# Some feed-forward block pairs of a three-product float32 kernel computed by Strassen's seven half-sized products

## The chip, the core and the metric

The kernel runs on one core of one Trainium2 chip. The metric is the device time of one execution in microseconds (us): the median of three runs of the kernel before is 2325.37 us (2324.46 to 2325.86).

## What is computed

The reference takes x (1 x 512 x 1024, float32) through a first block (RMSNorm, attention, gates, and an MLP with a squared ReLU, 1024 to 4096 to 1024) and through two layers of feed-forward, mixer, feed-forward. The feed-forwards are SwiGLUs of width 1408:

```
x = x + jnp.square(jax.nn.relu(h2 @ w_up[l])) @ w_down[l]      # the MLP

def _swiglu(u, wi, wo):
    a, g = jnp.split(u @ wi, 2, axis=-1)
    return (jax.nn.silu(a) * g) @ wo                           # four calls, u = rms_norm(x)
```

## The kernel before

Activations lie with features on the partitions and the 512 positions along the row, in eight feature blocks (k = 0 to 7). A float32 product is made of three: each operand is split into a high part (`xh`, `whi`, a cast) and a low part (`xl`, `wlo`, the difference), and `mm3` (L389) issues high by high, high by low, low by high into one bank of PSUM.

A weight tile is loaded raw by SyncE's queue (`wraw`, 2 buffers, L382), cast by ScalarE into `whi` (L384, 4 buffers) and subtracted by VectorE into `wlo` (L385). The norm of a row enters late: the products run on x times its gain, and each result is multiplied by the row `Rrow` (L467) once `norm_job` (L496) has made it from a sum of squares (`ssq`), a reciprocal root and two helper products (`dg`, `bcps`); results that are ready sooner are held.

`swiglu` (L570) makes 11 blocks j of 128 features. Each loads two chunks of weights (k 0 to 3 and 4 to 7), multiplies into `pa` and `pg` with `fm` (24 matmuls of 512 columns each), and hands over to an evacuation: VectorE `t1` (L582) and `t2` (L584), ScalarE Silu (L583), GpSimd `t2 * t1` (L585), then ScalarE's cast `hidh` (L562) and VectorE's difference `hidl` (L563). `mlp` (L609) works in three groups of 11, 11 and 10 blocks, two blocks to a load, with `pu` and a square (L625 to L628), and after each group `down` (L592) multiplies by the second matrix into `pd` and adds to x (L480). `down` is the last reader of a group's `hid` places, which come from a store `H` of 22 places of 4 KB a row. Scratch tiles (`scr`) rotate through 6 places, PSUM through 8 banks.

TensorE runs in the order in which the program is written, with other jobs put in at `turn()`. The order of the other engines is set by the scheduler at build time; each of them then runs its own list in order.

Of the kernel before, what the change touches and what calls it, by code (L numbers as in the profile page):

```python
# [28 lines left out]
def dram(t, off, ap):  # L29
    return bass.AP(tensor=t.tensor, offset=t.offset + off, ap=ap)  # L30
# [125 lines left out]
class Net:  # L156
# [44 lines left out]
        return self.ps.tile([128, S], F32, name=name, tag="ps")  # L201


    def mm(self, out, lhsT, rhs, start, stop):
        self.nc.tensor.matmul(out, lhsT, rhs, start=start, stop=stop)  # L205
        n = 1
        for d in rhs.shape[1:]:
            n *= d
        self.loom.now += n * 4.17e-4 if rhs.dtype == F32R else 2 * max(0.107, n * 8.34e-4)
# [176 lines left out]
            out += [(hi[:, k * w_:(k + 1) * w_], lo[:, k * w_:(k + 1) * w_]) for k in range(kn)]  # L386
        return out

    def mm3(self, ps, whi, wlo, xhi, xlo, first, last):  # L389

        self.mm(ps, whi, xhi, first, False)
        self.mm(ps, whi, xlo, False, False)
        self.mm(ps, wlo, xhi, False, last)

    def mm3t(self, ps, whi, wlo, xhi, xlo, first, last):

# [146 lines left out]
    def square(self, tb, t, ssq):  # L543
        A = self.nc.scalar
        junk = self.H.get("xj", [128, D])
        A.activation(junk, t, AF.Square, accum_out=ssq[:, tb:tb + 1])
        self.H.put(junk, t)

    def x_tok_job(self, out):
        for tb in range(TB):  # L550
            yield lambda: self.H.room(4096)
            t = self.H.get("xtok", [128, D])
            for h in range(2):
                ps = self.bank("xtp")
                for k in range(4):
                    self.tr(ps[:, k * 128:(k + 1) * 128], self.x[:, h * 4 + k, tb * 128:(tb + 1) * 128], self.ident)
                self.nc.scalar.copy(t[:, h * 512:(h + 1) * 512], ps)
            out.append(t)
            yield 10.0

    def split_to(self, hi, lo, t):
        self.nc.scalar.copy(hi, t)  # L562
        self.nc.vector.tensor_sub(lo, t, hi.bitcast(F32))  # L563


    def hid(self, n):
        hp = [self.pair("hid") for _ in range((n + 1) // 2)]
        return hp, self.blocks(hp, n)

    def swiglu(self, wi):  # L570
        nc = self.nc
        hp, hid = self.hid(11)
        for j in range(11):
            parts = self.load_w(wi, 2 * FFN, 0, KB, j * 128, 128, FFN + j * 128)
            pa, pg = self.bank("pa"), self.bank("pg")
            self.fm(parts, self.xs, 0, pa)
            self.fm(parts, self.xs, 1, pg)

            def evac(j=j, pa=pa, pg=pg):
                t1 = self.scr("t1")  # L580
                t2 = self.scr("t2")
                nc.vector.tensor_mul(t1, pa, self.rrow)  # L582
                nc.scalar.activation(t1, t1, AF.Silu)  # L583
                nc.vector.tensor_mul(t2, pg, self.rrow)  # L584
                nc.gpsimd.tensor_mul(t2, t2, t1)  # L585
                self.split_to(hid[j][0], hid[j][1], t2)
            self.hold(evac)
        return hp, hid

    def down(self, hid, wo, r0, scale, norm):  # L590
        n = len(hid)
        for c in range(4):  # L592
            parts = self.load_w(wo, D, r0, n, c * 256, 256)
            for i in range(2):
                ps = self.bank("pd")
                self.fm(parts, hid, i, ps)
                self.update_x(2 * c + i, ps, scale, norm)

    def down_tok(self, hid, wo, out, xtok):
        nc = self.nc  # L600
        for c in range(2):
            def evac(b, ps):
                o = self.scr("oo")
                cs = slice(c * 512, c * 512 + 512)
                nc.vector.scalar_tensor_tensor(o, ps, 0.5, xtok[b][:, cs], op0=ALU.mult, op1=ALU.add)
                nc.sync.dma_start(out[0, b * 128:(b + 1) * 128, cs], o)
            self.tm(wo, D, 0, hid, c * 512, 512, evac)

    def mlp(self, wu, wd, g_next):  # L609
        nc = self.nc  # L610
        j0 = 0
        for gi, n in enumerate((11, 11, 10)):
            hp, hid = self.hid(n)
            j = 0
            while j < n:
                w = min(2, n - j)
                parts = self.load_w(wu, 4096, 0, KB, (j0 + j) * 128, 128 * w)
                for i in range(w):
                    ps = self.bank("pu")
                    self.fm(parts, self.xs, i, ps)  # L620

                    def evac(ps=ps, hi=hid[j + i][0], lo=hid[j + i][1]):
                        r = self.scr("r")
                        q = self.scr("rq")
                        nc.vector.scalar_tensor_tensor(r, ps, 0.0, self.rrow, op0=ALU.max, op1=ALU.mult)  # L625
                        nc.gpsimd.tensor_mul(q, r, r)
                        nc.scalar.activation(hi, r, AF.Square)
                        nc.vector.tensor_sub(lo, q, hi.bitcast(F32))  # L628
                    self.hold(evac)
                j += w  # L630
            if gi == 2:
                self.g = g_next
            self.down(hid, wd, j0 * 128, 1.0, gi == 2)
            self.H.put(*sum(hp, ()))
            j0 += n

# [126 lines left out]
    def block1(self):  # L763
# [82 lines left out]
        def two(c0, c1, order, tabs, keys):  # L846

            ts = [self.tok("qk") for _ in range(2)]

            def ev(b, ps):  # L850
                for i in range(2):
                    nc.scalar.activation(ts[i][:, b], ps[:, i * 256:i * 256 + 256], AF.Copy,
                                         scale=rc[:, order * 4 + b:order * 4 + b + 1])
            self.tm(w, IN_WIDTH, 0, self.xs, c0, 256, ev, order, c1)
            for i in range(2):
                heads(ts[i], order, tabs[i], keys[i], T_HEADS[i])
# [212 lines left out]
    def ffn2(self, l, which, g_next, last=False):  # L1069
        a = self.a  # L1070
        wi, wo = a[f"ffn{which}_wi_2"][l], a[f"ffn{which}_wo_2"][l]
        xtok = []
        if which == 1:
            b = a["b_in_2"][l]
            self.lcols = self.columns("lcols", [(dram(b, 0, []), 2), (dram(b, 256, []), 2), (dram(b, 768, []), 8),
                                                (dram(b, 3240, []), 24), (a["ml_conv_b_2"][l], 8), (a["ml_conv_w_2"][l], 32),
                                                (a["mla_q_norm_2"][l], 2), (a["mla_kv_norm_2"][l], 1)], 30.0)
        if last:
            self.loom.add(self.x_tok_job(xtok))
        hp, hid = self.swiglu(wi)  # L1080
        if last:
            self.loom.wait(lambda: len(xtok) == TB)
            self.down_tok(hid, wo, a["out"], xtok)
            return
        self.g = g_next
        self.down(hid, wo, 0, 0.5, True)
        self.H.put(*sum(hp, ()))
# [190 lines left out]
    def mla_job(self, l, c4t, c4, ssc, gq, gkv, y, ready):  # L1278
# [322 lines left out]
    def ml_attn(self, qkt, qk, wt, vml, got, ys, ready):  # L1601
# [33 lines left out]
        def fin():  # L1635
# [69 lines left out]
WB = (2, 4)  # L1705
```

## Time and profile before

| what | before |
|---|---|
| median of 3 runs | 2325.37 us |
| the profiled execution | 2324.79 us |
| its span, first to last instruction | 2323.1 us |
| TensorE busy | 2308.8 us, 99% |
| weight loads busy (beside the matmuls) | 1913.4 us, 82% |
| VectorE busy | 1293.6 us, 56% |
| ScalarE busy | 907.3 us, 39% |
| GpSimd busy | 381.3 us, 16% |
| granted TensorE clock | 1.0 of full |

The profile is one execution's record. An engine's busy share is an average over all stages; a wait that counts is one that ends last for TensorE. Matmuls overlap in the pipeline, so their pace is read from start to start and not from the length of one.

### The profile page before, as it was taken

To read this page: it belongs to the slowest core of one execution; us is meant where nothing else is said; L and a number is where in the kernel's file an instruction comes from. 1 tells how busy PE (TensorE), PEld (TensorE's weight loads), DVE (VectorE), ACT (ScalarE), POOL (GpSimd) and SP (SyncE) were. 2 spreads that over 40 slices of the span, in tenths; PEclk is the share of its full clock that TensorE was granted. 3 is DMA by queue.
4 is the path that set the end of the run, shared out by engine and by line. 5 is a ranking of instruction groups with operands and counts; after the bars stand their busy time and mean duration, and the time that the engine had idled before them with its cause. 6 is when DMAs were issued, how large, how long until landed. Compare 5 with 4: busy or idle time off the path is not lost.

```text
span 2323.1 us, 28438 instructions
## 1 busy us (share of the span) xinstructions
PE 2308.8 (99%) x10884; PEld 1913.4 (82%) x10884; DVE 1293.6 (56%) x2255; ACT 907.3 (39%) x1509; POOL 381.3 (16%) x385
## 2 busy tenths in 40 slices
PE   8999999999999999999999999999999999999999
PEld 7898888888888888877888888888888778888887
DVE  7844556444355545678564555455457674646552
ACT  6655432222223233656533333223236672333331
POOL 2000024101022112111111311211211101213110
PEclk9999999999999999999999999999999999999999
DMA  4223333233323323313323333333233142323332
GB/s 139 65 64 87 105 100 93 91 99 101 98 86 105 99 89 95 102 55 91 105 64 91 109 91 91 100 92 100 91 102 91 46 114 73 88 83 105 93 100 87
DMA packets 250524, 213.68 MB, mean 92 GB/s; under 512 B 14230, under 2 KB 234132, under 8 KB 250388
## 3 DMA queue, kind: packets, MB, share of 16 engines
q1 hardware_dynamic: 250388, 211.87, 30.6%
q8 instruction: 85, 1.39, 0.2%
q14 instruction: 51, 0.42, 0.1%
HBM read 208.64 MB, written 3.19 MB: 91 GB/s over the span
## 4 chain that ended last, share of the span: by engine, by line
PE 98%; DVE 1%; DMA 0%; ACT 0%; issue 0%; SPq 0%; ACTq 0%
PE pgate L205 15%; PE pd L205 15%; PE pt L205 14%; PE pg L205 10%; PE pa L205 10%; PE pu L205 8%; PE pf L205 6%; PE po L205 6%; PE pbr L205 5%; PE mls L205 1%; PE mnum L205 1%; PE sbl L205 1%; PE mss L205 1%; PE dio L205 1%; PE s L205 1%; PE pT L212 0%
## 5 line engine op out<-in xcount | busy, mean ns | idle before, releaser
L385 DVE TENSOR_TENSOR wlo<-wraw,whi 128x1024 fp32r<-128x1024 f32 (+3 forms) x394 | 550.8, 1398 | 414.1 <-ACT whi L384 409.8
L384 ACT CAST whi<-wraw 128x1024 fp32r<-128x1024 f32 (+3 forms) x394 | 404.3, 1026 | 657.2 <-PE pg L205 141.7
L205 PE MATMUL pd<-hidh,wlo 128*128 128x512 f32 x520 | 202.4, 389 | 0.0
L205 PE MATMUL pd<-hidl,whi 128*128 128x512 f32 x520 | 202.4, 389 | 0.0
L205 PE MATMUL pd<-hidh,whi 128*128 128x512 f32 x520 | 202.4, 389 | 0.0
L205 PE MATMUL pgate<-xh,whi 128*128 128x512 f32 x512 | 201.5, 394 | 0.0
L205 PE MATMUL pgate<-xh,wlo 128*128 128x512 f32 x512 | 199.6, 390 | 0.0
L205 PE MATMUL pgate<-xl,whi 128*128 128x512 f32 x512 | 199.4, 389 | 0.0
L205 PE MATMUL pt<-whi,xh 128*128 128x512 f32 (+2 forms) x480 | 182.2, 380 | 0.1
L205 PE MATMUL pt<-whi,xl 128*128 128x512 f32 (+2 forms) x480 | 172.5, 359 | 0.0
L205 PE MATMUL pt<-wlo,xh 128*128 128x512 f32 (+2 forms) x480 | 172.3, 359 | 0.0
L205 PE MATMUL pa<-xl,whi 128*128 128x512 f32 x352 | 137.3, 390 | 0.7 <-DVE xl L474 0.7
L205 PE MATMUL pa<-xh,whi 128*128 128x512 f32 x352 | 137.7, 391 | 0.0
L205 PE MATMUL pg<-xh,whi 128*128 128x512 f32 x352 | 137.5, 391 | 0.0
L205 PE MATMUL pa<-xh,wlo 128*128 128x512 f32 x352 | 137.2, 390 | 0.0
L205 PE MATMUL pg<-xh,wlo 128*128 128x512 f32 x352 | 137.1, 390 | 0.0
L205 PE MATMUL pg<-xl,whi 128*128 128x512 f32 x352 | 137.1, 389 | 0.0
L585 POOL TENSOR_TENSOR t<-t,t 128x512 f32<-128x512 f32 x44 | 56.8, 1290 | 426.5 <-ACT whi L384 303.8
L205 PEld LDWEIGHTS pd<-hidl,whi 128*128 128x128 f32 x520 | 97.6, 188 | 20.4
L205 PEld LDWEIGHTS pd<-hidh,whi 128*128 128x128 f32 x520 | 97.6, 188 | 20.2
L205 PEld LDWEIGHTS pd<-hidh,wlo 128*128 128x128 f32 x520 | 97.6, 188 | 20.1
L205 PEld LDWEIGHTS pt<-whi,xh 128*128 128x128 f32 x480 | 102.7, 214 | 13.0 <-issue 3.0
(519 smaller groups left out, 4612.8 us busy)
## 6 DMA issues: line engine op xcount, KB each, us to landing
wraw<-in_w_in_dram SPq DMA_DIRECT2D x116, 512.0 KB
wraw<-in_ffn_wi_dram SPq DMA_DIRECT2D x176, 256.0 KB
wraw<-in_ffn_wo_dram SPq DMA_DIRECT2D x34, 512.0 KB
wraw<-in_w_up_dram SPq DMA_DIRECT2D x32, 512.0 KB
wraw<-in_w_out_dram SPq DMA_DIRECT2D x24, 512.0 KB
wraw<-in_w_down_dram SPq DMA_DIRECT2D x24, 512.0 KB
wraw<-in_w_in_dram SPq DMA_DIRECT2D x32, 256.0 KB
wraw<-in_ffn_wo_dram SPq DMA_DIRECT2D x12, 384.0 KB
```

Of the source, the lines that this page charges most:

```text
L205: self.nc.tensor.matmul(out, lhsT, rhs, start=start, stop=stop)
L384: nc.scalar.copy(hi, raw)
L385: nc.vector.tensor_sub(lo, raw, hi.bitcast(F32))
L585: nc.gpsimd.tensor_mul(t2, t2, t1)
```

## The change

For 23 pairs of blocks the 48 matmuls of 512 columns are replaced by seven products of 12 matmuls of 256 columns. The two halves of the positions and the two halves of k make the quarters A11, A12, A21, A22 of the activations; two blocks c0 and c1 and the same halves of k make the four quarters of the weights. In a SwiGLU the pair is `pa` and `pg` of j = 3, 5, 7, 9; in the MLP it is two neighbouring blocks, seven times.

`forms` (once in each SwiGLU and once in the MLP, five calls) makes the four sums of activation quarters S2, N1, S3, S4 and splits them: per call 4 scaled copies on ScalarE (128x256), 16 scalar_tensor_tensor on VectorE (128x256), 8 casts and 8 differences (128x512). `load_sums` loads a pair's raw weights into two places of `H` of their own (`sraw`, not `wraw`), makes the sums `tA` and `tB` by four VectorE adds (128x512), and splits E11, E21 with E22, T2 with T4, and T1 with T3 into the four buffers of `whi` and `wlo`: 512 + 3 x 1024 columns where a pair had 2 x 1024. `seven` runs the products in the order A11 E11, S4 E22, A12 E21, S2 T2, A22 T4, N1 T1, S3 T3. The third adds into the bank of the first, and before it ScalarE copies that bank (`A.copy(s1, a)`, tile `m7`). Places for `hid` are taken pair by pair. In the last SwiGLU the transposes of x move to j = 10.

```diff
+    def forms(self):
+        nc, g, H = self.nc, self.g, self.H
+        V, A = nc.vector, nc.scalar
+        ng = self.tiny.tile([128, KB], F32, name="ng", tag="ng")
+        V.tensor_scalar(ng, g, -1.0, None, op0=ALU.mult)
+        names = ("S2", "N1", "S3", "S4")
+        self.sums = {n: tuple(H.get("sum" + n, [128, 4, 256], F32R) for _ in range(2)) for n in names}
+        half = slice(0, 256), slice(256, 512)
+        for i in range(2):
+            f = {n: self.scr("f" + n).rearrange("p (k c) -> p k c", c=256) for n in names}
+            t = self.scr("ft").rearrange("p (k c) -> p k c", c=256)
+            for j in range(2):
+                k1, k2 = 2 * i + j, 4 + 2 * i + j
+                x = lambda k, h: self.x[:, k, half[h]]
+                A.activation(t[:, j], x(k1, 1), AF.Copy, scale=g[:, k1:k1 + 1])
+                for n, k, h, sc, other in (("N1", k2, 1, g, t), ("S2", k1, 0, ng, f["N1"]), ("S3", k1, 0, g, t),
+                                           ("S4", k2, 0, ng, f["S2"])):
+                    V.scalar_tensor_tensor(f[n][:, j], x(k, h), sc[:, k:k + 1], other[:, j], op0=ALU.mult, op1=ALU.subtract)
+            for n in names:
+                hi, lo = (y[:, 2 * i:2 * i + 2] for y in self.sums[n])
+                self.split_to(hi, lo, f[n])
+        q = lambda k, h: [(self.xh[:, kk, half[h]], self.xl[:, kk, half[h]]) for kk in range(4 * k, 4 * k + 4)]
+        self.quarters = {"A11": q(0, 0), "A12": q(1, 0), "A22": q(1, 1)}
+        for n in names:
+            self.quarters[n] = [(self.sums[n][0][:, k], self.sums[n][1][:, k]) for k in range(4)]
...
+    def load_sums(self, w, ncol, c0, c1):
+        nc, H = self.nc, self.H
+        V, A = nc.vector, nc.scalar
+        E = []
+        for k0 in (0, 4):
+            raw = H.get("sraw", [128, 1024])
+            rv = raw.rearrange("p (k h c) -> p k h c", h=2, c=128)
+            for h, c in ((0, c0), (1, c1)) if c1 != c0 + 128 else ((None, c0),):
+                n = 128 if h is not None else 256
+                nc.sync.dma_start(rv[:, :, h] if h is not None else raw.rearrange("p (k c) -> p k c", c=256),
+                                  dram(w, k0 * 128 * ncol + c, [[ncol, 128], [128 * ncol, 4], [1, n]]))
+            E.append((raw, rv))
+        (r1, v1), (r2, v2) = E
+        ta, tb = (H.get(n, [128, 2, 4, 128]) for n in ("tA", "tB"))
+        V.tensor_add(ta[:, 1], v1[:, :, 1], v2[:, :, 1])
+        V.tensor_add(tb[:, 0], ta[:, 1], v1[:, :, 0])
+        V.tensor_add(tb[:, 1], tb[:, 0], v2[:, :, 0])
+        V.tensor_add(ta[:, 0], v1[:, :, 0], v1[:, :, 1])
+        out = {}
+        def split(src, n, names, pick):
+            hi = self.wp.tile([128, n], F32R, name="whi", tag="whi", bufs=WB[1])
+            lo = self.wp.tile([128, n], F32R, name="wlo", tag="wlo", bufs=WB[1])
+            self.split_to(hi, lo, src)
+            for i, name in enumerate(names):
+                out[name] = [tuple(y[:, o:o + 128] for y in (hi, lo)) for o in (pick(i, k) for k in range(4))]
+        flat = lambda t: t.rearrange("p a k c -> p (a k c)")
+        e11 = self.wp.tile([128, 512], F32R, name="whi", tag="whi", bufs=WB[1])
+        f11 = self.wp.tile([128, 512], F32R, name="wlo", tag="wlo", bufs=WB[1])
+        h11, l11 = (y.rearrange("p (k c) -> p k c", c=128) for y in (e11, f11))
+        A.copy(h11, v1[:, :, 0])
+        V.tensor_sub(l11, v1[:, :, 0], h11.bitcast(F32))
+        out["E11"] = [(e11[:, k * 128:k * 128 + 128], f11[:, k * 128:k * 128 + 128]) for k in range(4)]
+        split(r2, 1024, ("E21", "E22"), lambda i, k: k * 256 + i * 128)
+        split(flat(tb), 1024, ("T2", "T4"), lambda i, k: i * 512 + k * 128)
+        split(flat(ta), 1024, ("T1", "T3"), lambda i, k: i * 512 + k * 128)
+        H.put(ta, tb, r1, r2)
+        return out
...
+    def seven(self, w, ncol, c0, c1, u, v, done):
         nc = self.nc
-        hp, hid = self.hid(11)
+        V, A = nc.vector, nc.scalar
+        W = self.load_sums(w, ncol, c0, c1)
+        a, b, c, d, e = (self.bank("ps7")[:, 0:256] for _ in range(5))
+        m = self.scr("m7")
+        s1, u2 = m[:, 0:256], m[:, 256:512]
+        u3 = self.scr("u7")[:, 0:256]
+        def prod(ps, q, e, first):
+            for k in range(4):
+                self.mm3(ps, *W[e][k], *self.quarters[q][k], first and k == 0, k == 3, skip_group_check=not first)
+            self.loom.turn()
+        prod(a, "A11", "E11", True)
+        A.copy(s1, a)
+        prod(e, "S4", "E22", True)
+        prod(a, "A12", "E21", False)
+        prod(b, "S2", "T2", True)
+        V.tensor_add(u2, b, s1)
+        prod(d, "A22", "T4", True)
+        V.tensor_add(u2, e, u2)
+        prod(c, "N1", "T1", True)
+        V.scalar_tensor_tensor(v[:, 0:256], c, -1.0, u2, op0=ALU.mult, op1=ALU.subtract)
+        prod(b, "S3", "T3", False)
+        V.tensor_add(u3, b, s1)
+        V.scalar_tensor_tensor(v[:, 256:512], c, -1.0, u3, op0=ALU.mult, op1=ALU.subtract)
+        V.tensor_add(u[:, 256:512], d, u3)
+        done(a)
+    def swiglu(self, wi, last):
+        V, A, G = nc.vector, nc.scalar, nc.gpsimd
+        hp, hid = [], []
         for j in range(11):
+            self.more_hid(hp, hid, j + 1)
+            if j == 1:
+                self.forms()
+            if j in SEVEN:
+                self.loom.wait(lambda: self.normed)
+                t1, t2 = self.scr("t1"), self.scr("t2")
+                def done(c11, j=j, t1=t1, t2=t2):
+                    r = self.rrow
+                    V.tensor_mul(t1[:, 0:256], c11, r[:, 0:256])
+                    V.tensor_mul(t1[:, 256:512], t1[:, 256:512], r[:, 256:512])
+                    A.activation(t1, t1, AF.Silu)
+                    V.tensor_mul(t2, t2, r)
+                    G.tensor_mul(t2, t2, t1)
+                    self.split_to(hid[j][0], hid[j][1], t2)
+                self.seven(wi, 2 * FFN, j * 128, FFN + j * 128, t1, t2, done)
+                if j == SEVEN[-1]:
+                    self.drop_forms()
+                continue
...
+            if last and j > SEVEN[-1]:
+                last()
+                last = None
...
+                self.more_hid(hp, hid, j + w)
+                if gi == 0 and j == 2:
+                    self.forms()
+                if w == 2 and (gi, j) in SEVEN_MLP:
+                    self.loom.wait(lambda: self.normed)
+                    u, v = self.scr("u"), self.scr("v")
+                    def done(c11, j=j, u=u, v=v):
+                        r = self.rrow
+                        V.scalar_tensor_tensor(u[:, 0:256], c11, 0.0, r[:, 0:256], op0=ALU.max, op1=ALU.mult)
+                        V.scalar_tensor_tensor(u[:, 256:512], u[:, 256:512], 0.0, r[:, 256:512], op0=ALU.max, op1=ALU.mult)
+                        V.scalar_tensor_tensor(v, v, 0.0, r, op0=ALU.max, op1=ALU.mult)
+                        square(u, *hid[j])
+                        square(v, *hid[j + 1])
+                    c = (j0 + j) * 128
+                    self.seven(wu, 4096, c, c + 128, u, v, done)
+                    j += w
+                    continue
...
+SEVEN = (3, 5, 7, 9)
+SEVEN_MLP = {(0, 6), (1, 0), (1, 4), (1, 8), (2, 0), (2, 4), (2, 8)}
```

The first place at which the order moves is VectorE's list at the start of a SwiGLU (layer 0, first). `dg` ends the norm's chain, `wlo` is the second weight chunk of j = 2, and `Rrow` opens the held evacuations. Before:

```order
L457 TENSOR_TENSOR dg_5974<-ident_84,rcl_5969 128x512
L385 TENSOR_TENSOR wlo_6082<-wraw_6080,whi_6081 128x1024
L467 COPY Rrow_6019<-bcps_6016 128x512
L582 TENSOR_TENSOR t1_6021<-pa_5910,Rrow_6019 128x512
L584 TENSOR_TENSOR t2_6022<-pg_5911,Rrow_6019 128x512
```

and now, without the 18 lines between (the other sums of `forms`):

```order
L457 TENSOR_TENSOR dg_6461<-ident_84,rcl_6456 128x512
L597 SCALAR_TENSOR_TENSOR fN1_6486<-x_77,gains_327,ft_6489 128x256 x2
...
L563 TENSOR_TENSOR sumS3_6482<-fS3_6510,sumS3_6481 128x512
L563 TENSOR_TENSOR sumS4_6484<-fS4_6511,sumS4_6483 128x512
L467 COPY Rrow_6562<-bcps_6559 128x512
L385 TENSOR_TENSOR wlo_6627<-wraw_6625,whi_6626 128x1024
L714 TENSOR_TENSOR t1_6564<-pa_6397,Rrow_6562 128x512
```

All of `forms`, and `Rrow` too, now stand ahead of that chunk's `wlo`.

The second place is ScalarE's list around a seven in the same SwiGLU. Before, behind a block's end (`t1` is the Silu):

```order
L384 CAST whi_6437<-wraw_6436 128x1024
L384 CAST whi_6444<-wraw_6443 128x1024
L562 CAST hidh_5888<-t2_6357 128x512
L583 ACTIVATE t1_6428<-t1_6428 128x512
```

and now, at a seven (`whi_7346` is T1 with T3, `hidh_7246` the block before it, `m7_7355` the copy of the first product):

```order
L562 CAST whi_7342<-tB_7329 128x1024
L562 CAST whi_7346<-tA_7328 128x1024
L562 CAST hidh_7246<-t2_7313 128x512
L664 COPY m7_7355<-ps7_7350 128x256
L384 CAST whi_7458<-wraw_7457 128x1024
```

The copy that the third product waits for stands behind the `hidh` cast of the block before. At the first seven of a SwiGLU a cast of the next block's weights stands between as well, and on VectorE the add that begins `tB` of the next pair follows `t2` at once.

The third place is VectorE's list where the second group of the MLP begins with a seven. Before (`x` takes the last `pd` of the group, the `wlo` are the next group's):

```order
L385 TENSOR_TENSOR wlo_5145<-wraw_5143,whi_5144 128x1024
L385 TENSOR_TENSOR wlo_5213<-wraw_5211,whi_5212 128x1024
L480 TENSOR_TENSOR x_77<-pd_5092,x_77 128x512
L385 TENSOR_TENSOR wlo_5219<-wraw_5217,whi_5218 128x1024
L625 SCALAR_TENSOR_TENSOR r_5174<-pu_5149,Rrow_3682 128x512
```

and now:

```order
L480 TENSOR_TENSOR x_77<-pd_4405,x_77 128x512
L624 TENSOR_TENSOR tA_4483<-sraw_4479,sraw_4481 128x512
L627 TENSOR_TENSOR tA_4483<-sraw_4479 128x512
L625 TENSOR_TENSOR tB_4484<-tA_4483,sraw_4479 128x512
L480 TENSOR_TENSOR x_77<-pd_4440,x_77 128x512
L626 TENSOR_TENSOR tB_4484<-tB_4484,sraw_4481 128x512
L641 TENSOR_TENSOR wlo_4490<-sraw_4479,whi_4489 128x512
```

The first low part of the new group (`wlo_4490`, E11) stands behind the adds and behind the update of x that waits for the group's last product. The `sraw` places are those of the old group's first `hid` pair, so that their loads wait for the last matmul that reads it.

## Rows read from the trace of the kernel before

**Rows 1.** The page: engines over the span, granted clock by slice, chain by engine.

```profile
PE 2308.8 (99%) x10884; PEld 1913.4 (82%) x10884; DVE 1293.6 (56%) x2255; ACT 907.3 (39%) x1509; POOL 381.3 (16%) x385
...
PEclk9999999999999999999999999999999999999999
...
PE 98%; DVE 1%; DMA 0%; ACT 0%; issue 0%; SPq 0%; ACTq 0%
```

**Rows 2.** Timeline of TensorE, third SwiGLU block, layer 0: start us, took us, instruction.

```profile
752.27 0.39 PE L205 MATMUL pa<-xh,whi 128*128 128x512 f32 x1
...
754.99 0.39 PE L205 MATMUL pa<-xh,whi 128*128 128x512 f32 x1
...
755.44 0.39 PE L205 MATMUL pa<-xh,wlo 128*128 128x512 f32 x1
...
759.98 0.39 PE L205 MATMUL pg<-xl,whi 128*128 128x512 f32 x1
```

**Rows 3.** Timeline of TensorE, first projection: 256 columns, 21 matmuls in a row.

```profile
17.02 0.28 PE L205 MATMUL pt<-whi,xh 128*128 128x256 f32 x1
17.14 0.28 PE L205 MATMUL pt<-wlo,xh 128*128 128x256 f32 x1
...
19.41 0.28 PE L205 MATMUL pt<-whi,xl 128*128 128x256 f32 x1
```

**Rows 4.** Timeline of the weight loads in that projection.

```profile
16.66 0.19 PEld L205 LDWEIGHTS pt<-wlo,xh 128*128 128x128 f32 x1
```

**Rows 5.** Groups by shape: xcount | busy us, mean ns | idle before.

```profile
L385 DVE TENSOR_TENSOR wlo<-wraw,whi 128x1024 fp32r<-128x1024 f32 x356 | 514.1, 1444 | 363.6 <-ACT whi L384 359.3 <-PE mqp L205 3.4 <-issue 0.2
...
L683 DVE CUSTOM_DVE_ANT_0 p<-s,band 128x256 f32<-128x256 f32 x36 | 13.7, 420 | 2.3 <-PE s L205 2.3
L1578 DVE SCALAR_TENSOR_TENSOR mlqk<-cvt,lcols,mlqk 128x510 f32<-128x510 f32 x16 | 12.0, 749 | 0.4
...
L562 ACT CAST hidh<-t 128x512 fp32r<-128x512 f32 x44 | 27.4, 623 | 55.2 <-POOL t L585 55.2
...
L942 ACT COPY og<-dio 128x256 f32<-128x256 f32 x12 | 4.5, 372 | 14.9 <-PE dio L205 14.9
...
L585 POOL TENSOR_TENSOR t<-t,t 128x512 f32<-128x512 f32 x44 | 56.8, 1290 | 426.5 <-ACT whi L384 303.8 <-DVE t L584 65.3 <-ACT t L583 57.5
```

**Rows 6.** Timeline of VectorE at the norm of the first SwiGLU, layer 0.

```profile
742.37 0.68 DVE L457 TENSOR_TENSOR dg<-ident,rcl 128x512 fp32r<-128x512 f32 x1
742.98 1.22 DVE L385 TENSOR_TENSOR wlo<-wraw,whi 128x1024 fp32r<-128x1024 f32 x1
...
745.08 0.69 DVE L582 TENSOR_TENSOR t<-pa,Rrow 128x512 f32<-128x512 f32 x1
745.68 0.68 DVE L584 TENSOR_TENSOR t<-pg,Rrow 128x512 f32<-128x512 f32 x1
```

**Rows 7.** Timeline of three engines behind the second block, whose product ends at 752.27.

```profile
752.29 1.05 ACT L384 CAST whi<-wraw 128x1024 fp32r<-128x1024 f32 x1 [1.67 <-PE pg L205]
752.47 0.69 DVE L584 TENSOR_TENSOR t<-pg,Rrow 128x512 f32<-128x512 f32 x1 [0.59 <-PE pg L205]
...
753.30 1.29 POOL L585 TENSOR_TENSOR t<-t,t 128x512 f32<-128x512 f32 x1 [5.50 <-DVE t L584]
753.37 2.30 DVE L385 TENSOR_TENSOR wlo<-wraw,whi 128x1024 fp32r<-128x1024 f32 x1 [0.21 <-ACT whi L384]
...
754.62 0.62 ACT L562 CAST hidh<-t 128x512 fp32r<-128x512 f32 x1 [1.29 <-POOL t L585]
```

**Rows 8.** One 512 KB weight load: issue, the waiting cast, traffic by microsecond.

```profile
452.28 0.37 SPq L382 DMA_DIRECT2D wraw<-in_w_down_dram  x1
...
455.75 1.05 ACT L384 CAST whi<-wraw 128x1024 fp32r<-128x1024 f32 x1 [2.25 <-DMA wraw<-in_w_down_dram]
...
453.00:454.00 1.00, 1.00 (x6) 0.82 (x5) 0.47 (x1) 0.50 (x1) 0.00 (x0) 1.00 0.46 126
454.00:455.00 1.00, 1.00 (x6) 0.83 (x5) 0.60 (x2) 0.00 (x0) 0.00 (x0) 1.00 1.03 365
```

More of the change, by code (lines that the diff above doesn't have):

```diff
@@ L201, in bank, with mm @@
         return self.ps.tile([128, S], F32, name=name, tag="ps")
-    def mm(self, out, lhsT, rhs, start, stop):
-        self.nc.tensor.matmul(out, lhsT, rhs, start=start, stop=stop)
+    def mm(self, out, lhsT, rhs, start, stop, **k):
+        self.nc.tensor.matmul(out, lhsT, rhs, start=start, stop=stop, **k)
         n = 1
@@ L387, in load_w, with mm3 @@
         return out
[L389 to L393, printed above, removed]
+    def mm3(self, ps, whi, wlo, xhi, xlo, first, last, **k):
+        self.mm(ps, whi, xhi, first, False, **k)
+        self.mm(ps, whi, xlo, False, False, **k)
+        self.mm(ps, wlo, xhi, False, last, **k)
     def mm3t(self, ps, whi, wlo, xhi, xlo, first, last):
@@ L558, in x_tok_job @@
             out.append(t)
-            yield 10.0
+            yield 5.0
     def split_to(self, hi, lo, t):
@@ L563, in split_to, with more_hid @@
         self.nc.vector.tensor_sub(lo, t, hi.bitcast(F32))
[L566 to L570, printed above, removed]
-        nc = self.nc
-        hp, hid = self.hid(11)
-        for j in range(11):
+    def more_hid(self, hp, hid, n):
+        while len(hid) < n:
+            hp.append(self.pair("hid"))
+            hid += self.blocks(hp[-1:], 2)
+    def forms(self):
[23 more added lines that the diff above has]
+            self.quarters[n] = [(self.sums[n][0][:, k], self.sums[n][1][:, k]) for k in range(4)]
@@ new lines, in drop_forms @@
+    def drop_forms(self):
+        self.H.put(*sum(self.sums.values(), ()))
+    def load_sums(self, w, ncol, c0, c1):
[35 more added lines that the diff above has]
+        return out
@@ new lines, in swiglu @@
+    def swiglu(self, wi, last):
+        nc = self.nc
+        V, A, G = nc.vector, nc.scalar, nc.gpsimd
+        hp, hid = [], []
+        for j in range(11):
+            self.more_hid(hp, hid, j + 1)
[16 more added lines that the diff above has]
+                continue
@@ L581, in evac @@
                 t2 = self.scr("t2")
[L582 to L585, printed above, removed]
+                V.tensor_mul(t1, pa, self.rrow)
+                A.activation(t1, t1, AF.Silu)
+                V.tensor_mul(t2, pg, self.rrow)
+                G.tensor_mul(t2, t2, t1)
                 self.split_to(hid[j][0], hid[j][1], t2)
             self.hold(evac)
-        return hp, hid
+        return hp, hid[0:11]
     def down(self, hid, wo, r0, scale, norm):
@@ L602, in evac @@
             def evac(b, ps):
+                self.loom.wait(lambda: len(xtok) > b)
                 o = self.scr("oo")
@@ L610, in mlp, with square @@
         nc = self.nc
+        V, A, G = nc.vector, nc.scalar, nc.gpsimd
         j0 = 0
         for gi, n in enumerate((11, 11, 10)):
-            hp, hid = self.hid(n)
+            hp, hid = [], []
             j = 0
+            def square(r, hi, lo):
+                q = self.scr("rq")
+                G.tensor_mul(q, r, r)
+                A.activation(hi, r, AF.Square)
+                V.tensor_sub(lo, q, hi.bitcast(F32))
             while j < n:
                 w = min(2, n - j)
+                self.more_hid(hp, hid, j + w)
[15 more added lines that the diff above has]
+                    continue
                 parts = self.load_w(wu, 4096, 0, KB, (j0 + j) * 128, 128 * w)
@@ L620, in mlp, with evac @@
                     self.fm(parts, self.xs, i, ps)
-                    def evac(ps=ps, hi=hid[j + i][0], lo=hid[j + i][1]):
+                    def evac(ps=ps, hl=hid[j + i]):
                         r = self.scr("r")
[L624 to L628, printed above, removed]
+                        V.scalar_tensor_tensor(r, ps, 0.0, self.rrow, op0=ALU.max, op1=ALU.mult)
+                        square(r, *hl)
                     self.hold(evac)
@@ L631, in mlp @@
             if gi == 2:
+                self.drop_forms()
                 self.g = g_next
-            self.down(hid, wd, j0 * 128, 1.0, gi == 2)
+            self.down(hid[0:n], wd, j0 * 128, 1.0, gi == 2)
             self.H.put(*sum(hp, ()))
@@ L1077, in ffn2 @@
                                                 (a["mla_q_norm_2"][l], 2), (a["mla_kv_norm_2"][l], 1)], 30.0)
+        hp, hid = self.swiglu(wi, last and (lambda: self.loom.add(self.x_tok_job(xtok))))
         if last:
[L1079 to L1082, printed above, removed]
             self.down_tok(hid, wo, a["out"], xtok)
```

## The prediction

> **What bounds the kernel now.** I read the page first. TensorE is busy 99% of the span at the full granted clock, and the chain that ended last lies on it for 98% [rows 1]: time is won by issuing fewer columns, and lost wherever TensorE must wait. Then TensorE's timeline, for its pace. From 752.27 to 759.98 lie 34 starts of 512 columns, 226.8 ns each [rows 2]. From 17.02 to 19.41 lie 20 starts of 256 columns, each with a new weight load, 119.5 ns each [rows 3]. Last the timelines of the other engines at the places where the change adds waits; their numbers come with their terms.
>
> The profiled execution took 2324.79 us, 0.6 below the median of the runs; I sum against it.
>
> **What TensorE saves.** A pair was 48 x 0.2268 = 10.88 us. Seven products are 84 x 0.1195 = 10.04 us. That is 0.84 us a pair, and 23 pairs give 19.3 us. Columns alone (21504 for 24576) would give 1/8, or 1.36; the 36 more starts take the rest back. A load's 188 ns overlap the matmuls at this pace [rows 4].
>
> Here the Trainium skill speaks against the change: "TensorE: Matmul & The Clock Gate", section "Back-to-back issue gap", says that load and matmul together set the spacing, and gives 81 ns at 128 and 131 ns at 512 columns. A straight line between them gives an estimate of 98 ns at 256, by which seven products (8.2 us) would cost more than 48 matmuls (6.3 us), and the 23 pairs would lose 44 us. The trace's two paces are others, and I take them.
>
> **What the new waits cost.** T is the end of the block ahead of a seven, the start of its first product; a product takes 12 x 0.1195 = 1.43 us, and the third starts at T+2.87 if nothing waits.
>
> *Forms, five starts.* VectorE ends `dg` at 742.37 + 0.60 = 742.97; back to back its 512-column operations start 0.60 us apart though each lasts 0.69 [rows 6]. A 256-column operation lasts 0.42, one of 512 with a gain column 0.749 in place of 0.69 [rows 5], so a step of the 16 scalar_tensor_tensor is some 0.42 + 0.055 - 0.09 = 0.385. With 8 differences at 0.60 `forms` takes 6.2 + 4.8 = 11.0 us, to 753.95. `Rrow` (0.60) and the chunk's `wlo` (1.23) follow: 755.8, and with 0.1 to TensorE 755.9. Two hand-overs with ScalarE inside, such as the idle 0.21 in [rows 7], may add one such gap: 756.1. TensorE needs the chunk at 755.44 [rows 2]. I take 0.7 each, 3.5 us. Ends: 0, if the 256-column steps are 0.335 and no gap shows; 2.65, if each operation takes its full duration. The evacuations held until `Rrow` cost nothing, since their banks are wanted only at the seven, 8 us later.
>
> *The copy in twelve later SwiGLU sevens.* Behind a block that ends at 752.27, `t2` starts at 752.47, GpSimd's product at 753.30, the `hidh` cast at 754.62 for 0.62 [rows 7]: the cast ends at T+2.97. The copy now stands behind it on ScalarE and lasts 0.37 [rows 5], to T+3.25 with the overlap of steps, T+3.35 with the hand-over. The third product waited from T+2.87: 0.47 each, 5.6 us. Ends 0.2 and 0.6.
>
> *The copy in the first sevens, five.* Here the add for `tB` follows `t2` on VectorE, from T+0.80 to T+1.49, with two operands in SBUF. In [rows 7] the `wlo` difference lasts 2.30 us where it starts 0.07 behind GpSimd's 1.29 us product, and 1.23 elsewhere: whichever of the two comes second waits. So GpSimd's product comes at T+1.5, the cast ends at T+3.45, the copy reaches TensorE at T+3.9: 1.0 each, 5.0 us. Ends 0.47 (no delay) and 1.5.
>
> *The copy in four MLP sevens, (1,4), (1,8), (2,4), (2,8).* Ahead of it stands a 1024-column cast that waits for the first product (T+1.43): from T+1.65 to T+2.65, the copy to T+3.0, TensorE at T+3.1. I take 0.27, 1.1 us in all. Ends 0 and 0.5.
>
> *Two groups of the MLP that begin with a seven, (1,0) and (2,0).* The raw places come free when the old group's last output (33 matmuls) has done its sixth, 27 x 0.2268 = 6.1 us ahead of T. One 512 KB load went from issue to cast in 3.47 us, at 365 GB/s in its full microsecond (the last column of the windows) [rows 8], so the second one needs 1.44 us more: both are there at T-1.1. Three adds (1.8) run to T+0.75, the update of x, the last add and E11's difference (1.8) to T+2.55, TensorE goes on at T+2.65. It wanted that low part at T+0.24 plus the 0.1 of its start: 2.3 each, 4.6 us. Ends 0.7 and 3.3 (the second load only as long again as the first).
>
> Nothing is charged for the casts and differences of 1.5 x 1024 more columns a pair: VectorE and ScalarE have idle time beside TensorE (56% and 39% busy), and what they make is wanted from the second product on, with whole blocks between. If that cover were gone, 1.23 us a difference would show. The moved transposes of x are as many as before.
>
> **Sum.** -19.3 + 3.5 + 5.6 + 5.0 + 1.1 + 4.6 = +0.5: 2325.3 us. A measurement of this kernel tells 0.2%, 4.65 us, from no change, so this is no change. The low ends (0, 2.4, 2.35, 0, 1.4) sum to 6.2 of waits, the high ends (13.3, 7.2, 7.5, 2.0, 6.6) to 36.6.
>
> **The rivals.**
> 1. *The waits mostly fit.* Each term has its low end: 2324.8 - 19.3 + 6.2 = 2311.7 us, faster. For it: all five are short tails of a chain that is late by 0.3 to 2.3 us, and in the kernel before such chains end in time everywhere (TensorE 98% of the chain). Against: the copy's place behind `hidh` is fixed by the order.
> 2. *GpSimd loses the port at every seven* (slower). In [rows 7] GpSimd's product starts only 0.07 us ahead of VectorE's difference. Where the T1 and T3 difference starts first, GpSimd waits 1.2 us, the cast, the copy and the third product with it, in the twelve SwiGLU sevens: 12 x 1.2 = 14.4, 2339.7 us. It decides at 0.07 us; before, the four blocks that follow `Rrow` in this SwiGLU kept GpSimd first. The Trainium skill ("SBUF — State Buffer", section "SBUF: two separate sides") says that whichever starts first holds the shared ports for its whole instruction, as this rival needs; the 2.30 agrees.
> 3. *Forms and raw weights at their high ends* (slower). 5 x 1.95 + 2 x 1.0 = 11.8 more: 2337 us. For it: the mean `wlo` is 1444 ns, not 1230 [rows 5]. Against: in [rows 6] the steps are the shorter ones.
> 4. *256 columns don't keep their pace* (the change doesn't save what it says). At 10.88 / 84 = 129.5 ns the products save nothing: 2344.6 us. Against: 119.5 over 20 steps, with a load for each. The figures of the Trainium skill above lean this way; the trace gives it little.
>
> **Chances.** Forecast 0.38, rival 1 0.33, rival 2 0.12, rival 3 0.12, rival 4 0.05. Faster by over 0.2% (under 2320.7): 0.31 from rival 1 and 0.05 from the forecast's low side, 0.36. Slower (over 2330.0): 0.29 from the last three rivals and 0.07 from the forecast, 0.36. The rest, 0.28, within 0.2%. The forecast's own range is 2319 to 2332. The one that should hold 8 in 10 reaches from rival 1 to rivals 2 and 3, 2311 to 2341, and leaves out what lies below rival 1's ends and rival 4.
>
> **What would show it.** Right: products of 12 matmuls 119.5 ns apart; per SwiGLU, TensorE idle behind a `wlo` once (some 0.7 us), behind the copy of `m7` four times (1.0, then 0.47); idle of 2.3 us behind VectorE at (1,0) and (2,0). Wrong: no idle behind `m7` (rival 1); GpSimd's product starting behind a `wlo` at each seven (rival 2); idle over 2 us at j = 2 (rival 3); a pace of 130 ns (rival 4); or TensorE idle at a place not named here, the next block's weights behind a seven above all.

## The result, and the profile after

The changed kernel takes 2353.95 us (median of 4 runs, 2353.58 to 2355.63) against 2325.6 us before: 1.0123 times, 95% interval 1.0111 to 1.0135. It is slower by 28.4 us, where 2325.3 was forecast and the range ended at 2341.

The page of the changed kernel, the lines that answer to [rows 1]:

```profile
PE 2308.1 (98%) x11712; PEld 1944.6 (83%) x11712; DVE 1468.9 (62%) x2679; ACT 977.9 (42%) x1638; POOL 398.6 (17%) x385
...
PEclk9999999999999999999999999999999999999999
```

TensorE is busy as long as before, though it streams fewer columns, and VectorE 175 us longer. The clock line still reads 9 everywhere, but the mean granted clock fell from 1.000 to 0.997; the tenths hide it.

What TensorE waited for (engine, tile and line, releaser: us in total, times, longest). The kernel before has four such groups: `colT` 4.4 and `xtp` 4.2 at the program's start, `pT` 1.2, and `xl`, once:

```profile
PE pa L205 <- DVE xl L474: 0.7, 1, 0.7
```

The changed kernel has thirteen, 40.1 us in all for 10.5; the seven largest:

```profile
PE ps L205 <- ACT m L664: 13.7, 17, 2.4
PE ps L205 <- DVE wlo L641: 5.2, 2, 2.6
PE colT L212 <- DMA rows<-in_ln_g_dram: 4.6, 1, 4.6
PE pa L205 <- DVE xl L474: 4.5, 2, 2.6
PE xtp L212 <- DMA xin<-in_x_dram: 4.1, 1, 4.1
PE pa L205 <- DVE wlo L385: 2.5, 3, 1.0
PE bcps L205 <- DVE dg L457: 1.8, 3, 0.8
```

So 17 of 23 sevens waited for the copy `m7`, two for E11's low part (`wlo` L641), and the starts of the SwiGLUs for `xl`, `wlo` and `dg`.

The starts of a quiet seven (MLP (1,4)), first matmul, last of the second product, first two of the third, and the next block:

```profile
529.44 0.28 PE L205 MATMUL ps<-xh,whi 128*128 128x256 f32 x1
...
532.20 0.28 PE L205 MATMUL ps<-sumS,wlo 128*128 128x256 f32 x1
532.37 0.39 PE L205 MATMUL ps<-xh,whi 128*128 128x256 f32 x1
532.60 0.28 PE L205 MATMUL ps<-xl,whi 128*128 128x256 f32 x1
...
539.66 0.40 PE L205 MATMUL pu<-xh,whi 128*128 128x512 f32 x1
```

It lasts 10.22 us. All steps are 0.12 but two at the third product, where the copy is only just in time. A later SwiGLU seven (j = 5):

```profile
797.96 0.28 PE L205 MATMUL ps<-xh,whi 128*128 128x256 f32 x1
...
801.29 0.39 PE L205 MATMUL ps<-xh,whi 128*128 128x256 f32 x1 [0.30 <-ACT m L664]
...
808.58 0.40 PE L205 MATMUL pa<-xh,whi 128*128 128x512 f32 x1
```

Its third product starts at T+3.33, as forecast (T+3.35), and the seven lasts 10.62 us. The idle shown is 0.30, the loss 0.55 against a seven without a wait (10.07, below): a matmul that waited costs some 0.25 beyond its idle. Of that, 0.16 lie in the reading: idle counts from the last matmul's end, 0.28 behind its start, where the next would have started 0.12 behind it. The other 0.10 are the step behind the wait, 0.22 in place of 0.12.

At the first seven (j = 3, T = 774.59) VectorE, GpSimd, ScalarE and TensorE:

```profile
773.43 1.28 DVE L563 TENSOR_TENSOR hidl<-t,hidh 128x512 fp32r<-128x512 f32 x2
774.63 1.21 DVE L563 TENSOR_TENSOR wlo<-tB,whi 128x1024 fp32r<-128x1024 f32 x1
775.77 0.68 DVE L624 TENSOR_TENSOR tA<-sraw 128x512 f32<-128x512 f32 x1
776.37 0.68 DVE L716 TENSOR_TENSOR t<-pg,Rrow 128x512 f32<-128x512 f32 x1
776.97 0.68 DVE L625 TENSOR_TENSOR tB<-tA,sraw 128x512 f32<-128x512 f32 x1
777.57 2.28 DVE L563 TENSOR_TENSOR wlo<-tA,whi 128x1024 fp32r<-128x1024 f32 x1
...
777.22 1.55 POOL L717 TENSOR_TENSOR t<-t,t 128x512 f32<-128x512 f32 x1 [4.79 <-ACT whi L384]
...
778.81 0.62 ACT L562 CAST hidh<-t 128x512 fp32r<-128x512 f32 x1 [1.65 <-POOL t L717]
779.33 0.36 ACT L664 COPY m<-ps 128x256 f32<-128x256 f32 x1
...
779.75 0.39 PE L205 MATMUL ps<-xh,whi 128*128 128x256 f32 x1 [2.02 <-ACT m L664]
```

`t2` starts at T+1.78, not at T+0.20 as in [rows 7]: two `hidl`, the low part of T2 with T4 and an add stand ahead of it. GpSimd, `hidh`, the copy and the third product (T+5.16) are late by 1.6 to 1.8. In the other three SwiGLUs `t2` starts at T+1.21, 1.59 and 1.14, and there GpSimd's product begins 0.25 behind VectorE's T1 and T3 difference and lasts 2.08 in place of 1.29, so that the third products start at T+5.12, 5.49 and 5.05. In the second one:

```profile
1392.83 1.21 DVE L563 TENSOR_TENSOR wlo<-tA,whi 128x1024 fp32r<-128x1024 f32 x1
1393.08 2.08 POOL L717 TENSOR_TENSOR t<-t,t 128x512 f32<-128x512 f32 x1 [4.27 <-DVE t L716]
```

At the twelve later sevens `t2` starts at T+0.20, and GpSimd's product 0.05 ahead of that difference. In the MLP's first seven the copy stands behind a `hidh` that waited 2.21 us for VectorE's `r`, and behind a cast of the next block's weights.

The start of the same SwiGLU on VectorE, with GpSimd's products and TensorE's wait:

```profile
738.99 0.68 DVE L480 TENSOR_TENSOR x<-pd,x 128x512 f32<-128x512 f32 x1
739.59 0.68 DVE L625 TENSOR_TENSOR tB<-tA,sraw 128x512 f32<-128x512 f32 x1
740.31 1.41 DVE L626 TENSOR_TENSOR tB<-tB,sraw 128x512 f32<-128x512 f32 x1
741.64 2.29 DVE L385 TENSOR_TENSOR wlo<-wraw,whi 128x1024 fp32r<-128x1024 f32 x1
743.85 0.74 DVE L474 SCALAR_TENSOR_TENSOR xl<-x,gains,xh 128x512 fp32r<-128x512 f32 x1
...
739.75 1.42 POOL L487 TENSOR_TENSOR sqk<-x 128x512 f32<-128x512 f32 x1 [5.92 <-DVE x L480]
741.25 1.60 POOL L491 TENSOR_TENSOR sqa<-sqa,sqk 128x512 f32<-128x512 f32 x1
...
744.65 0.50 PE L205 MATMUL pa<-xl,whi 128*128 128x512 f32 x1 [2.57 <-DVE xl L474]
```

Between the update of x and the last `xl` stand two adds for the first seven's `tB`, and beside GpSimd's products one lasts 1.41 and the chunk's low part 2.29 (1.97 in the kernel before). TensorE waits 2.57 us, where the kernel before waited 0.7.

The clock, by stretches around a wait in the third SwiGLU (us, then busy time of PE, PEld, DVE, ACT, POOL, granted clock, DMA share, GB/s):

```profile
1540.00:1546.00 6.00, 4.11 (x19) 3.11 (x18) 4.70 (x6) 1.67 (x2) 2.33 (x2) 1.00 0.56 152
1546.00:1549.50 3.50, 3.50 (x9) 2.72 (x9) 1.03 (x2) 0.00 (x0) 0.00 (x0) 0.51 0.93 272
1549.50:1553.00 3.50, 3.50 (x21) 2.98 (x20) 1.22 (x6) 1.04 (x1) 0.00 (x0) 1.00 0.61 165
```

and TensorE's timeline there:

```profile
1545.79 0.57 PE L205 MATMUL pa<-xl,whi 128*128 128x512 f32 x1 [1.89 <-DVE xl L474]
...
1546.58 0.63 PE L205 MATMUL pg<-xh,whi 128*128 128x512 f32 x1
1547.01 0.63 PE L205 MATMUL pg<-xl,whi 128*128 128x512 f32 x1
```

Behind a wait of 1.89 us TensorE ran at the lower level (1.2 GHz) for 3.4 us, 0.43 us a start of 512 columns, and lost half of that, 1.7 us. The trace has four such stretches inside the work, at 508, 1546, 1584 and 2201 us, each behind a wait of 1.9 to 2.6 us; the kernel before has none. Four other waits of 2.0 to 2.6 us, at 630, 745, 780 and 1396 us, were followed by none.

### The profile page after: what moved, and what is told of

It is laid out like the page before. It is cut to its first block, busy times and chain, and to the rows that moved or that the text cites. A ratio compares the mean times of both kernels' runs of the same rounds, so it can differ in the third digit from the quotient of the medians.

```text
span 2351.9 us, 30630 instructions
## 1 busy us (share of the span) xinstructions
PE 2308.1 (98%) x11712; PEld 1944.6 (83%) x11712; DVE 1468.9 (62%) x2679; ACT 977.9 (42%) x1638; POOL 398.6 (17%) x385
## 5 line engine op out<-in xcount | busy, mean ns | idle before, releaser
L385 DVE TENSOR_TENSOR wlo<-wraw,whi 128x1024 fp32r<-128x1024 f32 x348 | 441.4, 1268 | 288.3 <-ACT whi L384 284.2
L384 ACT CAST whi<-wraw 128x1024 fp32r<-128x1024 f32 x348 | 355.8, 1023 | 541.7 <-PE pd L205 103.0
L205 PEld LDWEIGHTS pd<-hidl,whi 128*128 128x128 f32 x520 | 97.6, 188 | 21.1 <-DVE hidl L754 0.8
L205 PEld LDWEIGHTS pgate<-xh,whi 128*128 128x128 f32 x512 | 96.1, 188 | 20.0
L205 PEld LDWEIGHTS pgate<-xh,wlo 128*128 128x128 f32 x512 | 96.1, 188 | 20.0
L205 PEld LDWEIGHTS pgate<-xl,whi 128*128 128x128 f32 x512 | 96.2, 188 | 19.6
L205 PEld LDWEIGHTS pt<-whi,xl 128*128 128x128 f32 x480 | 103.3, 215 | 8.3
L205 PEld LDWEIGHTS pt<-wlo,xh 128*128 128x128 f32 x480 | 103.8, 216 | 7.4 <-issue 0.5
L205 PE MATMUL ps<-sumS,whi 128*128 128x256 f32 x552 | 104.9, 288 | 0.0
L473 ACT ACTIVATE xh<-x,gains 128x512 fp32r<-128x512 f32 x56 | 40.4, 721 | 141.7 <-DVE x L480 75.1
```

The source lines that it names most:

```text
L384: nc.scalar.copy(hi, raw)
L385: nc.vector.tensor_sub(lo, raw, hi.bitcast(F32))
L473: nc.scalar.activation(hi, self.x[:, k], AF.Copy, scale=g[:, k:k + 1])
```

## The experiments

Two theories. W: the loss is TensorE's waits behind the new chains on VectorE and ScalarE, and the clock falls that follow the longer ones. P: the half-sized products keep a worse pace than 120 ns in this mix. All edits are to the changed kernel.

**1. The third product last.**

```diff
         prod(e, "S4", "E22", True)
-        prod(a, "A12", "E21", False)
...
         V.tensor_add(u[:, 256:512], d, u3)
+        prod(a, "A12", "E21", False)
         done(a)
```

> The product A12 E21 moves from third to last place, so that ScalarE's copy of the first product has seven products of time. Theory W (the loss is TensorE's waits behind the new chains, and the clock falls that follow the longer ones): the 17 waits for the copy (13.7 us idle, some 0.2 us more each to start again) go, and with two of them two stretches of 3.4 us at half clock: about 17 to 20 us less, 2334 to 2337 us; each SwiGLU seven lasts about 10.1 to 10.2 us. Rival P (256-column matmuls keep a worse pace than 120 ns in this mix, the waits only hide it): under 5 us less, 2349 us or more, sevens still at 10.6.

2332.89 us (1.0031, interval 1.0019 to 1.0043): 21.1 us less. The waits for the copy are gone, and only two clock falls are left, both at the MLP's group starts. A SwiGLU seven, first start and the next block's:

```profile
794.05 0.28 PE L205 MATMUL ps<-xh,whi 128*128 128x256 f32 x1
...
804.13 0.40 PE L205 MATMUL pa<-xh,whi 128*128 128x512 f32 x1
```

10.08 us by these rounded starts, 10.07 unrounded: the pace was as read in [rows 3], and P falls. A pair saves 10.88 - 10.07 = 0.81 us where nothing waits.

**2 and 3. Only the MLP's sevens, only the SwiGLUs'.**

```diff
-SEVEN = (3, 5, 7, 9)
+SEVEN = ()
```

(and no call of `forms` in a SwiGLU), or

```diff
-SEVEN_MLP = {(0, 6), (1, 0), (1, 4), (1, 8), (2, 0), (2, 4), (2, 8)}
+SEVEN_MLP = set()
```

(and none in the MLP).

> Only the seven pairs of the MLP, and no forms in the SwiGLUs. W: the MLP's share of the loss alone, 6 to 8 us by the shift of its stages (2.8, 2.4, 0.9 and one clock fall): about 2332 us. P: 7/23 of the loss, about 2334 us, with no wait to show for it. Rival D (VectorE's extra work delays all later stages): also stages without sevens are longer.

> Only the sixteen pairs of the SwiGLUs. W: the SwiGLUs' share, some 3.3 + 3.4 + 7.4 + 4.9 us and their starts, about 20 us: 2346 us. The two shares add up to the whole 28 us if no stage hands its delay on. P: 16/23 of the loss, 2345 us.

2334.78 us (1.0040, 1.0026 to 1.0055), 9.3 more than the 2325.5 before, and 2344.62 us (1.0082, 1.0067 to 1.0097), 19.1 more. They add up to 28.4, the whole loss: no stage hands its delay on. Stages without sevens are not longer either: from the start of the first SwiGLU's `down` (`pd`) to that of the last projection of the mixer behind it (`po`) lie 447.3 us in the kernel before (850.3 to 1297.6) and 447.3 in the change (862.5 to 1309.9). Rival D falls.

**4. No sevens at the group starts.**

```diff
-SEVEN_MLP = {(0, 6), (1, 0), (1, 4), (1, 8), (2, 0), (2, 4), (2, 8)}
+SEVEN_MLP = {(0, 6), (1, 4), (1, 8), (2, 4), (2, 8)}
```

> The change without the sevens that begin the MLP's second and third group, (1,0) and (2,0). W: two waits of 2.6 us for E11's low part go, and the clock fall behind the first; these sevens took 14.5 and 13.0 us against 10.9 for a plain pair: about 5 to 6 us less, 2348 us. P: the two pairs were no worse than others: 1 us less at most.

2345.4 us (1.0084, 1.0069 to 1.0099): 8.5 less, more than expected. The direction is W's; the size is beyond the two sevens. In the profiled executions it is 7.2 us: 6.3 in the MLP's second and third group, 0.7 at the program's start, and the rest of the kernel gives 0.2, since the clock falls there only stand at other places than in the change (739, 776 and 1394 us). The 1.3 us between that and the medians stay open.

**5. Edits 1 and 4 together.**

> Both edits together: the product A12 E21 last, and no sevens at the start of the MLP's second and third group. W: the two savings touch different places, so that they add: 2332.9 - 8.5 = 2324.4 us (2323 to 2327), no clock fall left in the MLP. Rival (the savings overlap, or something common to all sevens costs): 2328 us or more.

2326.62 us (1.0004, 0.9995 to 1.0014): as expected, the two savings add. The sevens now pay just for the waits that are left (`xl` 3.4, `wlo` 2.5, `dg` 1.8, and 4.2 of smaller ones) and one clock fall.

**6. The adds of the first seven held until the norm is there**, on top of 5.

```diff
-        V.tensor_add(ta[:, 1], v1[:, :, 1], v2[:, :, 1])
+        first = self.one is None
+        if first:
+            self.one = self.tiny.tile([128, 1], F32, name="one1", tag="one1")
+            V.tensor_scalar(self.one, self.rcol[:, 0:1], 0.0, 1.0, op0=ALU.mult, op1=ALU.add)
+            V.scalar_tensor_tensor(ta[:, 1], v1[:, :, 1], self.one, v2[:, :, 1], op0=ALU.mult, op1=ALU.add)
+        else:
+            V.tensor_add(ta[:, 1], v1[:, :, 1], v2[:, :, 1])
...
```

> As the run before, and the adds that make tA and tB of the first seven of each SwiGLU and of the MLP read a column made from the norm's result (times 0, plus 1), so that VectorE can't do them ahead of the last xl. W: at the starts of the first and third SwiGLU the wait for xl falls from about 1.9 and 2.4 to 0.7 or less, the waits for dg shrink: 4 to 6 us less than the run before, about 2319 us. Rival (xl is late for another reason, the copies of forms on ScalarE or the port that GpSimd holds): no gain, and the later adds make the first sevens wait.

2332.46 us (1.0031, 1.0018 to 1.0043): 5.8 more, a miss. The `xl` waits did fall, from 3.4 to 1.2 us (`dg` only from 1.8 to 1.6), but the adds then stood behind `forms`, and each first seven waited for E11's low part:

```profile
PE ps L205 <- DVE wlo L651: 10.1, 5, 5.6
...
PE pa L205 <- DVE xl L474: 1.2, 2, 0.8
```

**7. `forms` one block later**, on top of 5, **and 8. both.**

```diff
-            if j == 1:
-                self.forms()
...
             parts = self.load_w(wi, 2 * FFN, 0, KB, j * 128, 128, FFN + j * 128)
+            if j == 2:
+                self.forms()
```

(in the MLP behind the load of block 4.)

> As the first run of this call, and forms is called one block later, behind the loading of that block's weights: VectorE then does the chunk's low part and Rrow ahead of forms. W: the waits for that chunk's wlo (2.5 us in three SwiGLU starts) and the late evacuations go, 2 to 4 us less, about 2321 us. Rival (the first seven now waits for forms itself): waits for a sum's low part appear, no gain.

> The two edits of the last two runs together. W: 2324.4 less both savings, 2315 to 2319 us, faster than the kernel before by 0.3% or more: 21 pairs at 0.81 us are 17 us, less what is left at the starts. Rival (VectorE is full at the starts, a wait only moves): 2321 us or more.

2347.54 us (1.0094, 1.0079 to 1.0109) and 2341.28 us (1.0067, 1.0052 to 1.0082), 21 and 15 more than run 5: misses, on the side of the rival. In run 7 the first seven waited for the sums, five times each:

```profile
PE ps L205 <- DVE sumS L563: 5.6, 5, 1.1
PE ps L205 <- DVE wlo L563: 5.6, 5, 1.2
PE pa L205 <- DVE xl L474: 4.7, 2, 3.0
...
PE ps L205 <- ACT sumS L562: 2.1, 5, 0.5
```

and its trace has five places with a clock fall in the SwiGLUs and the MLP, each around a first seven. In each of the orders tried the first seven comes too soon behind the start of a SwiGLU: a wait put out at one place came back at another.

**9 to 11. The first sevens two blocks later.**

```diff
-SEVEN = (3, 5, 7, 9)
-SEVEN_MLP = {(0, 6), (1, 4), (1, 8), (2, 4), (2, 8)}
+SEVEN = (5, 7, 9)
+SEVEN_MLP = {(0, 8), (1, 4), (1, 8), (2, 4), (2, 8)}
```

on top of 8, of 7 and of 5; 17 pairs.

> The run with both edits, but the first seven of a SwiGLU at j = 5 and that of the MLP at (0,8), two blocks later: 17 pairs. W: forms, the held adds and the held evacuations now have 22 us more of cover, the waits at the first seven (sums, wlo: 15 us in that run) go: 17 x 0.81 = 13.8 us saved, some 1 to 3 us left for xl and dg: 2313 to 2316 us, faster than the kernel before by 0.4 to 0.5%. Rival (a late first seven only moves the jam): 2322 us or more.

> The same without holding the adds. W: VectorE's list has adds ahead of an xl again, which costs 3 to 4 us in two of the four SwiGLU starts: 2316 to 2319 us. Rival (the adds don't matter): the same as the run before within 1 us.

> The product A12 E21 last, no sevens at group starts, first sevens at j = 5 and (0,8), but forms as early in the program as in the change. W: forms stands ahead of the chunk's wlo again (2.5 us in three starts) and the adds ahead of xl: 2318 to 2321 us. Rival (forms early costs nothing once the first seven is late): as the run before.

2313.29 us (0.9949, 0.9936 to 0.9961), 2315.35 us (0.9959, 0.9945 to 0.9973) and 2318.34 us (0.9970, 0.9959 to 0.9981): all three beat the kernel before, the first by 12.2 us. Run 9 came out as expected. Run 10 shows no `xl` wait, so that its reason was wrong: with the first seven at j = 5 the adds stand behind the last `xl` even where they aren't held (728.33 behind 726.54 in the first SwiGLU). In the third they stand inside the norm's chain, and `dg` is waited for once, 1.9 us; but the profiled executions of runs 9 and 10 took the same (2314.3 and 2314.4), so that the 2.1 us between the medians, whose intervals overlap, are not explained by it. Run 11, within its range, has no `xl` wait either, but one of 1.7 for `dg`, three for `wlo` (1.2 in all), and a clock fall. It differs from run 5 in nothing but the first sevens' places: 8.3 us less. TensorE's waits of run 9 that are not the program's start:

```profile
PE ps L205 <- DVE m L677: 1.7, 2, 1.2
PE pT L212 <- DVE p L1065: 1.2, 1, 1.2
PE ps L205 <- DVE wlo L563: 0.4, 1, 0.4
```

and its span and mean granted clock:

```profile
core 0: 2312.6 us, clock 1.000
```

17 x 0.81 = 13.8 us saved, 2.1 us of new waits, no clock fall.

**12. The change with only the first sevens later** (the edit of 9 on the change itself, its group starts kept).

> The change with nothing altered but the first sevens: j = 5 in place of 3, (0,8) in place of (0,6); the copy stays ahead of the third product, forms stays early. W (the 1.6 to 2.4 us at the five first copies come from the evacuations that forms holds up, which stand on VectorE ahead of t2): two blocks later VectorE has caught up, every copy wait is 0.3 us, as at the later sevens: 12 to 16 waits of 0.3, 4 to 5 us in place of 13.7, and 2341 to 2345 us. Rival (the first copy is late whatever stands before it, by its place behind the cast of the next block's weights): first waits of 1 us or more at j = 5 too.

2333.39 us (1.0036, 1.0023 to 1.0049): 20.6 less, 8 more than expected. The copy, still ahead of the third product, now waits as the later sevens do everywhere:

```profile
PE ps L205 <- ACT m L664: 3.5, 12, 0.3
```

3.5 us in 12 waits of 0.3, in place of 13.7 in 17. The `xl` waits (4.5 us) went too, and so did all clock falls but one. The first seven of the first SwiGLU, now j = 5 (T = 791.06), has `t2` at T+0.20:

```profile
791.26 0.69 DVE L716 TENSOR_TENSOR t<-pg,Rrow 128x512 f32<-128x512 f32 x1 [0.59 <-PE pg L205]
...
793.45 0.62 ACT L562 CAST hidh<-t 128x512 fp32r<-128x512 f32 x1 [1.31 <-POOL t L717]
793.98 0.36 ACT L664 COPY m<-ps 128x256 f32<-128x256 f32 x1
```

The edit moved the rival's cast as well: it now follows the copy (794.24), where it stood ahead of `hidh` in the change. But there it was done 1.66 us before `hidh` began, and in the MLP, where it still stands ahead of the copy, the wait fell from 1.61 to 0.15. So the first copies were late for VectorE's backlog, not for their place.

## Why the prediction was wrong

By its own steps:

- *What TensorE saves*, 0.84 us a pair. Right: 0.81 without a wait (run 1), 18.6 for 19.3 in all.
- *Forms, five starts*, 0.7 each. Right: `forms` took 11.2 us (753.72 to 764.88) for 11.0; the waits are 2.5 us in three SwiGLU starts and 0.4 in the MLP, 2.9 for 3.5.
- *The copy in twelve later sevens*, 0.47 each. Right: the third product starts at T+3.33; with the slower step behind it, 0.55.
- *Four MLP sevens*, 0.27 each: 0.15.
- *Two group starts*, 2.3 each: 2.6 of idle. Near, but for the clock fall behind the first.
- *The copy in the first sevens*, 1.0 each, 5.0 us. Measured, in idle, 1.61, 2.02, 2.08, 2.36 and 2.02: 10.1 us. The step that failed is the sentence "The evacuations held until `Rrow` cost nothing, since their banks are wanted only at the seven, 8 us later." I looked for who needs the banks, and not for what the late evacuations push back on VectorE itself: their `hidl` and the seven's own low parts stand ahead of `t2`, which came 0.9 to 1.6 us later in the four SwiGLUs than the T+0.20 that the step took from [rows 7], a block without a backlog. The step had allowed some 0.5 for the port; in three SwiGLUs GpSimd's product lost 0.8 to the T1 and T3 difference on top of the late start. At the later sevens and in run 12, with the same low parts but no held evacuations, `t2` is in time. How much of the lateness is the held work itself and how much GpSimd's products, beside which a low part lasted 2.31 for 1.21 (771.20), no run parts.
- *Nothing is charged* for the added casts and differences, by VectorE's mean busy share; the adds of the first pair at a SwiGLU's start were in no term at all. Their raw places are free early, so that VectorE does them in the middle of the x updates: `xl` waited 4.5 us for 0.7, and run 6, which holds them, takes most of that back. `dg` waited 1.8 us for none, and run 6 still has 1.6, so that this part is not shown to be theirs. The same adds were charged at the MLP's group starts, where I had read the list.
- *No term for the clock.* Four falls of 1.7 us, 6.8 us, behind waits that the sum had only as long as themselves. Beside that TensorE kept the slow pace (0.21 us a start of 256 columns) 3.5 us longer at the program's start, at a price of 1.5, ahead of anything that the change touches.
- *No term for the slower step behind a wait*: 0.10, some 32 times, 3 us. The other 0.16 of the 0.25 the terms had, since they are delays of a start; beside them the idles above are each to be read 0.16 larger. The 0.25 holds for longer waits too: a seven of run 9 with a wait of 1.20 lasts 11.53, 0.26 beyond its idle.

Together, for the profiled execution: -18.6 saved, +29.6 more idle, +6.8 clock, +1.5 at the start, +8 for what 32 waits cost beyond their idle, 27.3 of the 28.9 us by which TensorE's last matmul came later. Some 1.6 us I can't place.

Of the rivals none was it. The waits did not fit (1), though run 9 shows how they can. At the twelve sevens of rival 2 GpSimd kept the port, by 0.05 us, and the copies came when forecast; it lost it at three first sevens, 0.8 us each. Forms stayed far from their high end, the group starts lay between the middle and theirs (3). The pace held (4). So the estimate from the figures of the Trainium skill ("TensorE: Matmul & The Clock Gate", "Back-to-back issue gap"), by which the 23 pairs lose 44 us, doesn't fit these matmuls, which start 0.12 and 0.227 us apart. The range was too narrow because its high end held only waits that I had named, and had no room for one I had not.

## What to carry to other kernels

A step that makes an engine late by 11 us is to be followed through everything that stands behind it in that engine's list, until it has caught up; the first user of the new scheme pays for the backlog, and moving that user two blocks back took off 8.3 us (run 11 against 5) and 28.0 us (run 9 against 8). With the third product last and no sevens at the group starts that was a gain; alone, in run 12, it left 8 us of loss. An algorithm that saves 7% of a block's matmul time has room for about one short wait per block: place the accumulating product where its copy can't be late, and count a wait by what it costs to start again and by the clock behind it, and not by its idle alone. A work list that a scheduler fills early (loads into free places) is read at the stage ahead of the one that uses it.

## What was not expected of the hardware

In the change TensorE fell to the lower clock for 3.4 us behind waits of 1.9 to 2.6 us, each time at a price of 1.7 us, but behind four others as long it didn't. The length of one wait is not all: at the five places of run 7 it fell around first sevens that waited three times each, 0.3 to 1.2 us. Falls differ between builds (one in run 5, none in run 9) and, by the mean clock, between executions of one build: in run 5 the three at 1.000 took 2324.3 to 2325.6 us, the seven at 0.999 2326.4 to 2329.2. What decides it stayed open.

A matmul that waited costs 0.25 us more than the idle that the trace shows for it.

In [rows 7] VectorE's difference lasts 2.30 us where GpSimd's product began 0.07 ahead of it. In the change the same is seen the other way: behind a difference that had begun 0.25 us earlier, GpSimd's product lasted 2.08 us in place of 1.29.
